# Joining the triangular inverses of two successive scan steps in one group of 64x64 products

## The chip, the cores and the metric

The kernel runs on one core of one Trainium2 chip. The metric is the time of one execution on the device in microseconds (us). A core has a matrix engine (PE, with its weight loads shown apart as PEld), a vector engine (DVE), a scalar engine (ACT), a general engine (POOL), and a queue processor (SP) that issues most of the transfers (DMA) between main memory and the on-chip memory. Each engine carries out its own list of instructions strictly in the order of that list. Matrix products end in PSUM, a memory of eight banks, from which DVE and ACT fetch them.

## The reference, cut to what matters

One layer mixes tokens in two ways, a gated delta rule and a windowed attention. The change lies in the delta rule. For each chunk of 64 tokens it needs the inverse of a unit lower triangular matrix, and then a scan over the chunks:

```python
a_mat = jnp.where(strict, jnp.einsum('nbhik,nbhjk->nbhij', kb, kc) * decay, 0.0)
t_mat = lax.linalg.triangular_solve(a_mat, eye, left_side=True, lower=True, unit_diagonal=True)
u = jnp.einsum('nbhij,nbhjv->nbhiv', t_mat, vc * bc[..., None])
w = jnp.einsum('nbhij,nbhjk->nbhik', t_mat, kb * jnp.exp(gc)[..., None])
def step(s, xs):
    v_new = u_n - jnp.einsum('bhck,bhkv->bhcv', w_n, s)
    s_new = s * jnp.exp(gl_n)[..., None, None] + jnp.einsum('bhck,bhcv->bhkv', kd_n, v_new)
    o = jnp.einsum('bhck,bhkv->bhcv', qd_n, s) + jnp.einsum('bhij,bhjv->bhiv', qk_n, v_new)
```

It runs forwards and backwards over 2048 latent tokens behind 256 context tokens, with 4 heads of 128 columns.

## The kernel before, in words

The kernel works on chunks of 128 tokens instead of 64, so the scan has 18 steps, each with a forward (d = 0) and a backward (d = 1) chain. DVE makes the inverses of the two 64x64 diagonal blocks of each 128x128 matrix earlier and spills them. `merge` joins two such inverses into one of 128x128 by the rule for block triangular matrices, which takes two 64x64 products per head and direction, one after the other: the off-diagonal block times the inverse of one diagonal block (line 1021 for d = 0 and 1023 for d = 1, into PSUM tiles `myp`), a scaling and copy out of PSUM (lines 1025 and 1026), and the inverse of the other block times that (lines 1028 and 1030, into `mep`), copied into place by ACT with a minus sign (lines 1032 and 1033).

In detail `merge` clears a tile `mx0` and a tile `mx1` on POOL (line 991), loads the diagonal inverses into them (line 1002) and the off-diagonal blocks into `moff0` and `moff1` (line 1004), and turns them by PE transposes into `mtp` (line 1011 for d = 0, whole; line 1013 for d = 1, the lower 64 rows alone). For d = 0 the result is the tile `mw`, for d = 1 it is `mx1` itself. `mx0`, `mx1`, `mw`, `moff0` and `moff1` have two buffers each. The helper `in_step` makes the four heads' products follow each other so that products which use different quarters of PE's 128x128 array stand side by side in PE's list: 64 rows by 64 columns each.

`chain` carries the state: `ksps` (line 1093), a DVE update of `x` (1095), `vps` = joined inverse times `x` (1099), DVE's `v3` (1102), `sps` (1111), and DVE's new state (1117). `output` makes the chunk's output (1135 to 1147), `finalize` its norm and gate. In `scan`, the chains of step `st` are written first, then `merge` for step `st + 1`, then the outputs. The last two steps' inverses come late, from `base4`, a DVE job that is spread over the scan.

The scan stands beside `gates`, dense products of 128x128 weights with 512 columns (lines 524 to 526, PSUM tile `rps`), which need nothing of the scan. A scheduler lays down every engine's list when the kernel is built: the scan is marked as urgent, and gate products are put where its chains would leave PE empty. What is left of them goes on into the next stage, the attention (scores `sc`, line 910; transposes `pt`; weighted sums `av`; a copy `avt`, line 951, ends a unit; 32 units), and the projections (`pps`, line 1231) follow, held back until the eighth unit is done.

## Time and profile before

| | us |
|---|---|
| median of 3 runs (2003.56 to 2009.0) | 2004.95 |
| profiled execution, first to last instruction | 2004.9 |
| first transposes of `merge` | 920.1 |
| last transposes of `finalize` | 1345.3 |
| first attention score | 1358.2 |
| last gate product | 1436.0 |
| first projection | 1481.1 |

The profile is one execution. A row of a timeline gives start, duration, engine, line, operation, the tiles written and read, the shape, the count, and in brackets the idle time before and what ended it. The durations of PE's products overlap, since a product is still in flight when the next one starts: what a product costs PE is the distance from its start to the next one's. A product of two plain fp32 tiles stands as two instructions in the profile, a transpose or a gate product as one. A row of windows gives the busy time of each engine in that stretch and, behind it, the clock that TensorE was granted.

### The profile page before, as it was taken

How to read it: one execution, taken by the hardware profiler on the slowest of the kernel's cores; microseconds unless marked ns; L12 is line 12 of the kernel's file. 1: busy time of each engine (PE TensorE's matmuls, PEld its weight loads, DVE VectorE, ACT ScalarE, POOL GpSimd, SP SyncE). 2: the span in 40 equal slices, each digit the busy share in tenths (PEclk: the TensorE clock that was granted, in tenths of full speed). 3: DMA queues.
4: the chain of work that ended last, by engine and by line, in shares of the span. 5: the costliest groups of instructions: out<-in, count | busy, mean ns of one | idle time of the engine just before them, and what ended most of it. 6: DMA issues, size and time to landing. Idle time of an engine off the chain costs nothing. (4 is left out here: it accounts for less than half of the span.)

```text
span 2004.9 us, 32107 instructions
## 1 busy us (share of the span) xinstructions
PE 1921.2 (96%) x10947; PEld 1611.0 (80%) x10947; DVE 1509.2 (75%) x2871; ACT 807.4 (40%) x1998; POOL 692.6 (35%) x768
## 2 busy tenths in 40 slices
PE   6999999989999999999999999999989999999998
PEld 3888888779998778877888888788768888877786
DVE  6979766667776899999777776535587777747888
ACT  5755545554444322111222233224675655532221
POOL 1652210225543202004222233323456444420675
PEclk8999999999999999999999999999999999999999
DMA  7542326764546733537887777755355555456454
GB/s 252 175 127 94 98 87 154 184 162 157 161 143 166 189 113 113 142 90 216 225 255 221 224 213 217 193 176 165 126 187 173 176 162 165 129 165 211 137 169 136
DMA packets 387704, 333.12 MB, mean 166 GB/s; under 512 B 83993, under 2 KB 307537, under 8 KB 386901
## 3 DMA queue, kind: packets, MB, share of 16 engines
q1 hardware_dynamic: 352244, 288.60, 49.9%
q10 hardware_dynamic: 35296, 42.48, 6.0%
q8 instruction: 87, 1.43, 0.3%
q14 instruction: 77, 0.62, 0.1%
HBM read 220.28 MB, written 109.13 MB: 164 GB/s over the span
## 5 line engine op out<-in xcount | busy, mean ns | idle before, releaser
L524 PE MATMUL rps<-hh,wh 128*128 128x512 f32 x768 | 309.6, 403 | 5.0 <-DVE rt L818 3.8
L526 PE MATMUL rps<-hh,wl 128*128 128x512 f32 x768 | 309.0, 403 | 0.0
L525 PE MATMUL rps<-hl,wh 128*128 128x512 f32 x768 | 307.7, 401 | 0.0
L563 DVE SCALAR_TENSOR_TENSOR cacc<-y,cw,cacc 128x512 f32<-128x512 f32 (+1 forms) x224 | 163.2, 750 | 22.9 <-ACT cacc L561 18.9
L524 PEld LDWEIGHTS rps<-hh,wh 128*128 128x128 f32 x768 | 145.7, 190 | 39.8 <-DVE rt L818 4.3
L525 PEld LDWEIGHTS rps<-hl,wh 128*128 128x128 f32 x768 | 145.8, 190 | 32.7
L526 PEld LDWEIGHTS rps<-hh,wl 128*128 128x128 f32 x768 | 145.7, 190 | 32.8
L524 PE MATMUL lps<-hh,wh 128*128 128x512 f32 (+1 forms) x448 | 171.6, 383 | 0.2 <-ACT y L634 0.2
L525 PE MATMUL lps<-hl,wh 128*128 128x512 f32 (+1 forms) x448 | 171.3, 382 | 0.0
L526 PE MATMUL lps<-hh,wl 128*128 128x512 f32 (+1 forms) x448 | 171.2, 382 | 0.0
L945 DVE TENSOR_TENSOR pl<-pt,ph 128x512 fp32r<-128x512 f32 x156 | 105.4, 685 | 41.9 <-ACT ph L943 41.2
L943 ACT CAST ph<-pt 128x512 fp32r<-128x512 f32 x156 | 90.2, 585 | 109.9 <-PE pt L941 76.8
L917 DVE CUSTOM_DVE_ANT_0 pr<-sc,band,sk 128x640 f32<-128x640 f32 (+1 forms) x128 | 106.6, 862 | 34.4 <-PE sc L913 18.3
L816 ACT ACTIVATE rt<-rps 128x512 f32<-128x512 f32 x96 | 57.3, 596 | 181.6 <-PE rps L526 167.8
L749 DVE TENSOR_TENSOR N<-N,btmp 128x62 f32<-128x62 f32 (+30 forms) x124 | 117.2, 945 | 3.0
L747 DVE TENSOR_TENSOR btmp<-N 128x62 f32<-128x62 f32 (+30 forms) x124 | 116.6, 940 | 3.1
L927 POOL TENSOR_SCALAR pr<-pr,sm 128x640 f32<-128x640 f32 (+1 forms) x128 | 99.7, 799 | 55.5 <-DVE sm L925 39.0
L919 ACT ACTIVATE pr<-pr,sm 128x640 f32<-128x640 f32 (+1 forms) x128 | 104.0, 815 | 20.4 <-DVE sm L917 20.4
L246 DVE TENSOR_TENSOR wl<-wr,wh 128x512 fp32r<-128x512 f32 x120 | 92.7, 786 | 24.7 <-POOL wh L245 21.9
L1231 PE MATMUL pps<-yh,wph 128*128 128x512 f32 x256 | 104.8, 411 | 4.3 <-ACT yh L1211 2.2
L245 POOL TENSOR_SCALAR wh<-wr 128x512 fp32r<-128x512 f32 x72 | 48.6, 690 | 170.3 <-PE lps L525 97.2
L1232 PE MATMUL pps<-yl,wph 128*128 128x512 f32 x256 | 100.9, 396 | 0.0
(374 smaller groups left out, 5044.2 us busy)
## 6 DMA issues: line engine op xcount, KB each, us to landing
wr<-in_w_in_dram SPq DMA_DIRECT2D x120, 256.0 KB
kw<-Ksp SPq DMA_DIRECT2D x28, 384.0 KB
x<-vsp SPq DMA_DIRECT2D x36, 256.0 KB
k<-ksp SPq DMA_DIRECT2D x34, 256.0 KB
kT<-kTsp SPq DMA_DIRECT2D x34, 256.0 KB
wm<-in_w_mod_dram SPq DMA_DIRECT2D x16, 512.0 KB
xt<-in_x_dram SPq DMA_DIRECT2D x16, 512.0 KB
dtl<-Dsp SPq DMA_DIRECT2D x32, 256.0 KB
```

Of the source, the lines that this page charges most:

```text
L524: T.matmul(ps, lhsT=wh[:, k], rhs=xh[:, k], start=k == 0, stop=False)
L525: T.matmul(ps, lhsT=wh[:, k], rhs=xl[:, k], start=False, stop=False)
L526: T.matmul(ps, lhsT=wl[:, k], rhs=xh[:, k], start=False, stop=k == kt - 1)
L563: V.scalar_tensor_tensor(a, y[:, t:t + n], cw[:, m, t:t + 1], a, op0=ALU.mult, op1=ALU.add)
L747: V.tensor_tensor(tv, A[:, m + 1:, m].unsqueeze(2).to_broadcast([h1 + n, r, m]), A[:, m, 0:m].unsqueeze(1).to_broadcast([h1 + n, r, m]), o ...
L749: V.tensor_tensor(A[:, m + 1:, 0:m], A[:, m + 1:, 0:m], tv, op=ALU.add)
L917: V.tensor_tensor_reduce(s_, ps[:, o:768], band[:, b0:b0 + W + 256], -0.125, sk[:, 1, hd:hd + 1], ALU.add, ALU.min, sm[:, h, 1:2])
L919: S.activation(s_, s_, AF.Exp, scale=-1.0, bias=sm[:, h, 1:2], accum_out=sm[:, h, 2:3])
L927: G.tensor_scalar(p[:, h, :W + 256], p[:, h, :W + 256], sm[:, h, 3:4], 1.0, op0=ALU.mult, op1=ALU.mult)
L945: V.tensor_tensor(pl, pt, f32(ph), op=ALU.subtract)
L1231: T.matmul(ps, lhsT=wh[:, k, ms], rhs=hs[k], start=k == 0, stop=False)
L1232: T.matmul(ps, lhsT=wh[:, k, ms], rhs=ls[k], start=False, stop=False)
```

## The change

`merge` is cut in two. `halves_of` does what came ahead of the first products: loads, transposes, the copy to `mw`, and for d = 1 the scaling (line 1014 now), which writes into a free part of `mx0` instead of a tile of its own. The d = 1 transposes are whole 128x128 ones now. `joined` then takes the second products of a step whose first are done (`done`) and the first products of the step after it (`begun`), and hands all four kinds to `in_step` as one group: `mep` in rows 0 to 63 of the array and one PSUM bank, `myp` in rows 64 to 127 and another bank. Behind it ACT copies the finished inverse into place, and DVE and ACT prepare the next. The scan therefore starts `halves_of` two steps ahead instead of one, with the same two buffers for each tile. No instruction of other functions changes.

```diff
-    def merge(pool, cs):
+    def halves_of(pool, cs):
...
             for h in hs:
-                if d == 0:
-                    T.transpose(tps[:, h], Xs[0][:, h], ident)
-                else:
-                    T.transpose(tps[:, h, 64:128], Xs[1][64:128, h], ident[64:128, 64:128])
+                T.transpose(tps[:, h], Xs[d][:, h], ident)
             tp.append(tps)
         brb = [br[:, c, d * 4:d * 4 + 4].unsqueeze(2).to_broadcast([128, H, 64]) for d, c in enumerate(cs)]
-        y0, y1 = offs[0], pool.tile([128, H, 64], F32, name="my1")
         W, X = pool.tile([128, H, 128], F32, name="mw", bufs=2), Xs[1]
         S.copy(W, tp[0])
-        V.tensor_tensor(y1[64:128], tp[1][64:128, :, 64:128], brb[1][64:128], op=ALU.mult)
-        yps = [psum(f"mg{d}", [128, H, 128], name="myp") for d in range(2)]
-        in_step([lambda h: T.matmul(yps[0][0:64, h, 0:64], lhsT=offs[0][64:128, h], rhs=W[64:128, h, 64:128],
-                                    start=True, stop=True),
-                 lambda h: T.matmul(yps[1][64:128, h, 0:64], lhsT=offs[1][64:128, h], rhs=y1[64:128, h],
-                                    start=True, stop=True)])
-        V.tensor_tensor(y0[0:64], yps[0][0:64, :, 0:64], brb[0][0:64], op=ALU.mult)
-        S.copy(y1[0:64], yps[1][64:128, :, 0:64])
-        eps_ = [psum(f"mg{d}", [128, H, 128], name="mep") for d in range(2)]
-        in_step([lambda h: T.matmul(eps_[0][0:64, h, 0:64], lhsT=Xs[0][0:64, h, 0:64], rhs=y0[0:64, h],
-                                    start=True, stop=True),
-                 lambda h: T.matmul(eps_[1][64:128, h, 0:64], lhsT=y1[0:64, h], rhs=X[0:64, h, 0:64],
-                                    start=True, stop=True)])
-        S.activation(W[0:64, :, 64:128], eps_[0][0:64, :, 0:64], AF.Copy, scale=-1.0)
-        S.activation(X[64:128, :, 0:64], eps_[1][64:128, :, 0:64], AF.Copy, scale=-1.0)
-        return W, X
+        xt2 = Xs[0][64:128, :, 64:128]
+        V.tensor_tensor(xt2, tp[1][64:128, :, 64:128], brb[1][64:128], op=ALU.mult)
+        return W, X, Xs[0], offs, xt2, brb
+
+    def joined(done, begun):
+
+        products = []
+        if done:
+            W, X, X0, offs0, _, _ = done
+            y0, y1 = (o[0:64] for o in offs0)
+            eps_ = psum("mg0", [128, H, 128], name="mep")
+            products += [lambda h: T.matmul(eps_[0:64, h, 0:64], lhsT=X0[0:64, h, 0:64], rhs=y0[:, h],
+                                            start=True, stop=True),
+                         lambda h: T.matmul(eps_[64:128, h, 0:64], lhsT=y1[:, h], rhs=X[0:64, h, 0:64],
+                                            start=True, stop=True)]
+        if begun:
+            W2, _, _, offs, xt2, brb = begun
+            yps = psum("mg1", [128, H, 128], name="myp")
+            products += [lambda h: T.matmul(yps[0:64, h, 0:64], lhsT=offs[0][64:128, h], rhs=W2[64:128, h, 64:128],
+                                            start=True, stop=True),
+                         lambda h: T.matmul(yps[64:128, h, 0:64], lhsT=offs[1][64:128, h], rhs=xt2[:, h],
+                                            start=True, stop=True)]
+        in_step(products)
+        if done:
+            S.activation(W[0:64, :, 64:128], eps_[0:64, :, 0:64], AF.Copy, scale=-1.0)
+            S.activation(X[64:128, :, 0:64], eps_[64:128, :, 0:64], AF.Copy, scale=-1.0)
+        if begun:
+            V.tensor_tensor(offs[0][0:64], yps[0:64, :, 0:64], brb[0][0:64], op=ALU.mult)
+            S.copy(offs[1][0:64], yps[64:128, :, 0:64])
...
-        W = merge(pool, [orders[d][0] for d in range(2)])
+        begun = halves_of(pool, [orders[d][0] for d in range(2)])
+        joined(None, begun)
+        done, begun = begun, halves_of(pool, [orders[d][1] for d in range(2)])
+        joined(done, begun)
         for st in range(NC):
+            W = done[:2]
             r = [chain(d, st, W[d]) for d in range(2)]
...
-            if st + 1 < NC:
-                W = merge(pool, [orders[d][st + 1] for d in range(2)])
+            done, begun = begun, halves_of(pool, [orders[d][st + 2] for d in range(2)]) if st + 2 < NC else None
+            if done:
+                joined(done, begun)
```

The scheduler's lists move with it. First place: PE's list in the middle of the scan, from the backward chain's `vps` to the transposes. The numbers behind `mx` tell the buffers' generations apart. Before:

```order
L1099 MATMUL vps<-x_10964,mw 128x128 x4
L1011 MATMUL mtp<-ident,mx_11038 128x128 x3
L1135 MATMUL aps<-S_10681,qT_10931 128x128 x4
L1099 MATMUL vps<-x_11002,mx_10868 128x128 x4
L1011 MATMUL mtp<-ident,mx_11038 128x128
L1013 MATMUL mtp<-ident,mx_11044 128x64 x4
```

And in the changed kernel, where 16 gate products stand in place of the line of dots:

```order
L1106 MATMUL vps<-x_11017,mx_10713 128x128 x4
L1008 MATMUL mtp<-ident,mx_11053 128x128 x4
...
L1153 MATMUL ops<-v_10865,qd_10948 128x128 x4
L1118 MATMUL sps<-v_10998,k_10977 128x128 x4
L1118 MATMUL sps<-v_11036,k_11015 128x128 x4
L1008 MATMUL mtp<-ident,mx_11059 128x128 x4
L1024 MATMUL mep<-moff_10884,mx_10880 64x64
L1026 MATMUL mep<-mx_10886,moff_10890 64x64
```

The d = 1 transposes (`mx_11059`) stood right behind `vps` and now stand 16 gate products, one `ops` and two `sps` later: their tile is the buffer that this very `vps` has just read (`mx_10713`). And one pair of `mep` products goes ahead of the group by itself.

Second place: PE's list at the groups of 64x64 products. Before, the second products of a step, eight together (its first products stand as such a group of eight a little earlier):

```order
L1093 MATMUL ksps<-S_11033,kT_11181 128x128 x2
L1028 MATMUL mep<-moff_11042,mx_11038 64x64
L1030 MATMUL mep<-mx_11044,my_11060 64x64
L1028 MATMUL mep<-moff_11042,mx_11038 64x64
L1030 MATMUL mep<-mx_11044,my_11060 64x64
...
L1146 MATMUL ops<-v_10985,qd_11090 128x128 x4
```

In the changed kernel, with two more rounds of the four in place of the dots:

```order
L1100 MATMUL ksps<-S_11048,kT_11193 128x128 x2
L1031 MATMUL myp<-mw,moff_11057 64x64
L1033 MATMUL myp<-mx_11053,moff_11063 64x64
L1024 MATMUL mep<-moff_10884,mx_10880 64x64
L1026 MATMUL mep<-mx_10886,moff_10890 64x64
...
L1031 MATMUL myp<-mw,moff_11057 64x64
L1033 MATMUL myp<-mx_11053,moff_11063 64x64
L1153 MATMUL ops<-v_11000,qd_11102 128x128 x4
```

Two groups of eight have become one of fourteen, behind a pair. In the whole list there were 41 unbroken runs of 64x64 products (36 groups, five of them with one product apart), and 18 blocks of 64-row transposes between whole ones; now there are 40 runs: 17 of fourteen, 13 pairs, 8 single products where a pair is broken by other work, and 2 groups of eight at the ends. The blocks of 64-row transposes are gone.

Third place: POOL's list, where the tiles are cleared ahead of their loads (line 989 now, 991 before; `x` times `rin` prepares the chains). Before:

```order
L1131 AFFINE_SELECT qd_11090<-qd_11090 128x512
L1086 TENSOR_TENSOR x_11140<-x_11140,rin 128x512
L991 MEMSET mx_11044 128x512
L1086 TENSOR_TENSOR x_11178<-x_11178,rin 128x512
L1131 AFFINE_SELECT qd_11109<-qd_11109 128x512
```

In the changed kernel:

```order
L1138 AFFINE_SELECT qd_11275<-qd_11275 128x512
L1093 TENSOR_TENSOR x_11325<-x_11325,rin 128x512
L989 MEMSET mx_11059 128x512
L1093 TENSOR_TENSOR x_11363<-x_11363,rin 128x512
L1138 AFFINE_SELECT qd_11294<-qd_11294 128x512
```

The place in POOL's list is the same, but `mx_11044` was read by transposes one step later, and `mx_11059` is read in the same step. Between the first transposes and the first attention score there are 991 gate products now, where there were 919; 120 are left behind that point, where there were 192. In the attention the last of them stands among the scores of the fifth unit of 32, where it was those of the seventh.

## The prediction

> **What bounds the kernel now.** I read the page's first part, then windows around the scan, then who waits for whom there. First the engines over the whole span:
>
> ```profile
> PE 1921.2 (96%) x10947; PEld 1611.0 (80%) x10947; DVE 1509.2 (75%) x2871; ACT 807.4 (40%) x1998; POOL 692.6 (35%) x768
> ```
>
> Then four windows, each with PE, PEld, DVE, ACT, POOL, the granted clock and DMA: the scan up to the first attention score, the attention while gate products last, four units of it without any, and two later units filled with projections:
>
> ```profile
> 920.00:1358.00 438.00, 427.35 (x3049) 369.60 (x3047) 298.37 (x707) 111.74 (x366) 139.95 (x218) 0.99 0.76 219
> 1358.00:1440.00 82.00, 81.97 (x440) 69.90 (x439) 47.19 (x109) 41.92 (x93) 28.37 (x35) 1.00 0.43 137
> 1440.00:1482.00 42.00, 34.86 (x184) 26.99 (x183) 34.25 (x77) 32.85 (x73) 26.64 (x27) 0.96 0.59 188
> 1550.50:1575.50 25.00, 25.00 (x144) 21.31 (x143) 18.34 (x42) 13.62 (x33) 11.01 (x12) 1.00 0.47 147
> ```
>
> PE is full wherever it has something to fill with. What it waits for in the scan:
>
> ```profile
> PE ksps L1093 <- DVE S L1117: 4.5, 1, 4.5
> PE ops L1146 <- DVE oa L1140: 1.8, 1, 1.8
> PE mep L1028 <- DVE moff L1025: 1.5, 1, 1.5
> ```
>
> These three are 7.8 us of 438. So the scan's chains set how long the stage is, gate products fill it, and a microsecond of PE's work saved there is worth one only if the filling left over is not missed later. The two windows of `rps` alone (counts of PEld, which has no missing records) tell how much fills each stage:
>
> ```profile
> 1358.00:1436.50 78.50, 48.85 (x194) 34.99 (x192) 0.00 (x0) 4.75 (x8) 1.00 0.42 132
> 920.00:1358.00 438.00, 241.52 (x921) 167.84 (x919) 10.20 (x15) 22.72 (x38) 0.99 0.76 219
> ```
>
> **The groups of 64x64 products.** A group between gate products in PE's timeline (start, duration):
>
> ```profile
> 925.53 0.40 PE L524 MATMUL rps<-hh,wh 128*128 128x512 f32 x1
> 925.77 0.39 PE L525 MATMUL rps<-hl,wh 128*128 128x512 f32 x1
> 926.09 0.27 PE L1021 MATMUL myp<-mw,moff 64*64 64x64 f32 x1
> 926.10 0.27 PE L1023 MATMUL myp<-my,moff 64*64 64x64 f32 x1
> 926.20 0.22 PE L1021 MATMUL myp<-mw,moff 64*64 64x64 f32 x1
> 926.20 0.22 PE L1023 MATMUL myp<-my,moff 64*64 64x64 f32 x1
> ...
> 926.55 0.22 PE L1021 MATMUL myp<-mw,moff 64*64 64x64 f32 x1
> 926.55 0.22 PE L1023 MATMUL myp<-my,moff 64*64 64x64 f32 x1
> 926.70 0.51 PE L526 MATMUL rps<-hh,wl 128*128 128x512 f32 x1
> 927.04 0.40 PE L524 MATMUL rps<-hh,wh 128*128 128x512 f32 x1
> ```
>
> A gate product takes 0.233 (925.53 to 925.77). From 925.77 to 927.04 are 1.27; less two gate products 0.80 for the group. Its eight slots, each with one instruction in either quarter, stand (926.55 - 926.20)/6 = 0.058 apart; so a run costs 0.33 for the change of mode and 0.058 per slot. Before: 41 runs, 36 x 8 slots and 10 more where one product stands apart, 298 slots: 41 x 0.33 + 298 x 0.058 = 30.8 us.
>
> Now there are 40 runs. That row and column quarters of different rows run at once no row shows: here both quarters share rows 64 to 127 and still start 0.01 apart. If four do as two do, the long runs take 8 slots (four `myp` rounds set them), pairs and single products 2: 17 x 8 + 21 x 2 + 2 x 8 = 194 slots, 24.5 us, 6.3 less. If pairs of different rows take turns, the long runs have 14 slots, 296 in all, 30.4 us, 0.4 less. I take the former, since one slot holds two quarters with hardly any of its 0.058 spent on the second.
>
> The Trainium skill has a rule against it: "TensorE: Matmul & The Clock Gate", section "Wait — 56ns, not 53.3ns?", says that starts never come closer than about 25 ns. By it a long run's 28 instructions would take 0.70 instead of 8 x 0.058 = 0.46, 4 us more in 17 runs, an estimate. The rows above, 0.01 apart and less, speak against it for different quarters.
>
> **The transposes.** Blocks of four and two, and the 64-row block that goes:
>
> ```profile
> 920.08 0.60 PE L1011 MATMUL mtp<-ident,mx 128*128 128x128 f32 x4
> 1139.79 0.38 PE L1011 MATMUL mtp<-ident,mx 128*128 128x128 f32 x2
> 1140.11 0.46 PE L1013 MATMUL mtp<-ident,mx 64*128 64x64 f32 x4
> 1140.49 0.50 PE L526 MATMUL rps<-hh,wl 128*128 128x512 f32 x1
> 1140.83 0.40 PE L524 MATMUL rps<-hh,wh 128*128 128x512 f32 x1
> ```
>
> A whole transpose costs (0.60 - 0.38)/2 = 0.11. The 64-row block costs 1140.83 - 0.233 - (1139.79 + 0.22) = 0.59; four whole ones cost 0.44. Over 18 blocks 2.7 us less. On DVE and ACT each instruction has a successor of the same size, so they change in order only.
>
> **Sum on PE:** 6.3 + 2.7 = 9.0 us less.
>
> **What it buys.** The two orders put 991 gate products before the first score instead of 919: 72 more, 72 x 0.233 = 16.8 us, taken from the attention. So the scan stage gets 16.8 - 9.0 = 7.8 longer, to about 446, and the attention starts as much later. It has 16.8 us less to fill with. A unit ends with a copy on ACT:
>
> ```profile
> L951 ACT COPY avt<-av x5: 583/584/587, 1440.1 to 1481.8; 64x512 f32<-64x512 f32 x5
> L951 ACT COPY avt<-av x3: 582/584/585, 1550.7 to 1575.2; 64x512 f32<-64x512 f32 x3
> ```
>
> Without filling a unit takes (1481.8 - 1440.1)/4 = 10.4. With 24 projection products of the gate products' size, PE full, it takes 12.25, so its own work is 12.25 - 5.6 = 6.7 and 3.7 us of PE are lost in a bare unit. Units with 24 gate products (the new order has 24 in each of the first three) stay full, as those projection units do. Then five bare units stand before the first projection where four stood: 3.7 us lost. At least none is lost, if the filling left over stretches; at most two units, 7.4. I take 3.7.
>
> **The load on the path.** `mx1` for step st + 2 takes the buffer that step st's `vps` reads, so clear, load and transposes now fit between that `vps` and the group on which the next step's inverse hangs. The same chain before, where it had a step's time, from DVE's reading of the finished `vps` to a load's arrival (POOL's multiply waits for one):
>
> ```profile
> 1100.77 0.69 DVE L1102 TENSOR_TENSOR v<-vps,brs 128x512 f32<-128x512 f32 x1 [0.20 <-PE vps L1099]
> 1100.77 0.32 SPq L1085 DMA_DIRECT2D x<-vsp  x1
> 1101.91 0.64 POOL L1131 TENSOR_SCALAR_AFFINE_SELECT qd<-qd 128x512 f32<-128x512 f32 x1 [7.13 <-DMA qd<-QDsp]
> 1102.49 0.53 POOL L991 MEMSET mx<- 128x512 f32 x1
> 1103.05 1.24 SPq L1002 DMA_DIRECT2D mx<-Xsp  x2
> 1103.90 1.04 POOL L1086 TENSOR_TENSOR x<-x,rin 128x512 f32<-128x512 f32 x1 [0.88 <-DMA x<-vsp]
> ```
>
> The clearing is done 2.3 after `vps`, the second load issued by 3.5; a load issued at 1100.77 was there at 1103.90 at the latest, 3.1 for four times the bytes. So 3.5 - 0.6 + 3.1 = 6.0 at most. The new order leaves four transposes, 16 gate products, an `ops` and two `sps`. Plain products cost:
>
> ```profile
> 1065.24 1.05 PE L1146 MATMUL ops<-v,qd 128*128 128x128 f32 x8
> 1066.13 1.95 PE L1111 MATMUL sps<-v,k 128*128 128x128 f32 x16
> ```
>
> (1.95 - 1.05)/8 = 0.11 each instruction, so the cover is 0.44 + 3.73 + 24 x 0.112 = 6.9. It just holds. I take 0.1 per step, 1.7 us: between nothing (it holds always) and 1 us per step (POOL's queue holds the clearing up). Queued behind the waiting clearing on POOL is `x` times `rin` of the next backward chain, behind the load on SP `qd` and the next `k`, all needed half a step later.
>
> The stalls of PE on DVE (7.8 us above) will be dealt out anew; they may all go or double. I take them as they are.
>
> **The sum:** 2004.9 (span; the median of the runs is 2004.95) - 9.0 + 3.7 + 1.7 = 2001.3 us.
>
> **Rivals.** *Taking turns:* quarters of different rows do not overlap; 5.9 us come back: 2007.2. For it, no row shows such an overlap; against it, the starts 0.01 apart. The issue floor of the Trainium skill's page on the clock gate, named above, would be a milder form of it, 2005.4 by the estimate there.
>
> *The load comes late* (the slower side): `mx1` is cleared late since POOL's list is blocked by a wait ahead of it, and PE's list waits at the d = 1 transposes in every step. For it:
>
> ```profile
> POOL qd L1131 <- DMA qd<-QDsp: 90.0, 23, 7.8
> ```
>
> POOL was blocked 23 times by this load alone, 3.9 on average. Against it: the memset's place behind `x` is unchanged, and in the list of PE's waits in this stage no load stands. It decides from the point where the clearing starts more than 6.9 - 0.5 - 0.6 - 3.1 = 2.7 after `vps` (1.7 here). A stall also costs clock. The only long one:
>
> ```profile
> 1269.86 2.08 PE L1093 MATMUL ksps<-S,kT 128*128 128x128 f32 x8 [4.46 <-DVE S L1117]
> 1269.00:1276.00 7.00, 6.14 (x23) 5.62 (x24) 6.05 (x19) 1.98 (x9) 5.47 (x9) 0.52 0.93 250
> ```
>
> Behind 4.5 us of waiting stood 7.0 us at 0.52, 3.4 lost. At 0.9 a step and one such loss of clock: 17 x 0.9 + 3.4 - 1.7 = 17 more, 2018.
>
> *Everything is bought:* the filling left over reaches as far as before and no unit is barer, the load always holds: 2001.3 - 3.7 - 1.7 = 1995.9. For it, units with few gate products are still above 10.4; against it, five whole units without filling in the new order.
>
> **Chances and range.** Forecast 0.58, taking turns 0.12, late load 0.16, all bought 0.14. A measurement tells 0.3%, 6.0 us, from no change: faster is below 1998.9, slower above 2011.0. The redealt stalls give the forecast some 5 us either way: 0.30 faster, 0.66 same, 0.04 slower. Taking turns: 0.05, 0.75, 0.20. Late load: none, 0.25, 0.75. All bought: 0.75, 0.25. That makes 0.29 faster, 0.55 same, 0.16 slower; the order of everything after the scan moves too, which no row prices, so I round towards the sides: 0.31, 0.50, 0.19. The range of 8 in 10 is 1993 to 2014: below it a part of all bought with luck in the stalls, above it most of late load.
>
> **What would show it.** Right: in a long run, four starts within 0.02 and rounds 0.12 apart; `mtp` 36 x 4 whole, no 64-row ones; first score near 1368 and 120 gate products behind it, the last ends near unit three; bare units of 10.4, five of them; first projection near 1477. Wrong: starts of `myp` and `mep` 0.06 apart (taking turns); idle time before `mtp` or `myp` put down to DMA or POOL (late load); a clock below 0.99 in the scan. A time off by more than 5 us with all of these right would mean that DVE's stalls, not PE's work, set this stage.

## The result, and the profile after

The changed kernel takes 2016.3 us in the median of 4 runs (2013.1 to 2016.5) where the kernel before took 2006.2 in 4 runs beside them: 1.0063 times as long, 95% interval 1.0046 to 1.0079. It got slower, where 2001.3 us was forecast and up to 2014 held possible. A repeat of both on another chip gave 1.0065 (1.0041 to 1.0088).

The profiled execution of the changed kernel, first part of its page:

```profile
span 2011.4 us, 32057 instructions
PE 1914.5 (95%) x10947; PEld 1603.1 (80%) x10947; DVE 1503.2 (75%) x2871; ACT 807.1 (40%) x1998; POOL 694.9 (35%) x768
```

This execution was the shortest of the four. PE is busy 6.7 us less than before (1921.2) and the span is 6.5 longer (2004.9): PE waits 13.2 us more. The windows by stage (length, then PE, PEld, DVE, ACT, POOL, granted clock, DMA), the scan first, then the attention up to the first projection, and the six units of it without gate products (their last 2.3 us hold first projections already):

```profile
919.00:1383.10 464.10, 440.45 (x3120) 379.78 (x3119) 293.47 (x710) 113.57 (x369) 146.04 (x223) 0.98 0.74 212
1383.10:1488.20 105.10, 99.66 (x545) 81.75 (x544) 78.62 (x180) 72.71 (x160) 52.13 (x57) 1.00 0.53 164
...
1433.90:1490.50 56.60, 51.16 (x281) 39.82 (x281) 51.92 (x114) 46.59 (x101) 35.77 (x38) 1.00 0.59 179
```

The scan is 464.1 us long (438.1 before) and PE idles 464.10 - 440.45 = 23.7 us in it (10.7 before). The attention up to the first projection is 105.1 (123.0 before). What follows is as long as it was: 523.2 against 523.8. So the loss lies in the scan. Gate products in the two stages, as forecast, 991 and 120 (column PEld):

```profile
919.00:1383.10 464.10, 263.94 (x992) 182.79 (x991) 10.19 (x15) 24.69 (x41) 0.98 0.74 212
1383.10:1431.00 47.90, 30.81 (x121) 21.68 (x120) 0.00 (x0) 2.98 (x5) 1.00 0.46 142
```

What PE waits for in the scan now, its own rows before `mtp` and the longest other one (sum, times, longest):

```profile
PE mtp L1008 <- DMA mx<-Xsp: 7.1, 6, 4.9
PE mtp L1008 <- POOL mx L996: 5.0, 2, 4.4
PE mtp L1008 <- POOL wh L245: 4.4, 1, 4.4
PE vps L1106 <- ACT mw L1037: 1.9, 1, 1.9
PE mtp L1008 <- POOL x L1093: 1.1, 1, 1.1
```

The transposes `mtp` at the head of `halves_of`, for which PE waited not once before, stand for 17.6 us in ten waits. Three of these, of 4.9, 4.4 and 4.4 us, make 13.7 of them; none of the others is longer than 1.1. By the tile that the transposes read (ACT's copy to `mw` follows those of `mx0`), 5.2 us fall to the load of `mx0`, 7.5 to that of `mx1` and 5.0 to copies of `base4`, the job that supplies the last steps' inverses. All other waits shrank from 10.2 to 5.8. The clock pays again for the long ones, in three stretches of the changed kernel's scan, where there were two in the scan before:

```profile
987.60:994.40 6.80, 5.58 (x16) 4.55 (x17) 0.69 (x1) 2.12 (x6) 2.04 (x2) 0.50 0.86 255
1028.60:1035.30 6.70, 5.77 (x17) 4.83 (x18) 6.33 (x17) 0.00 (x0) 3.26 (x4) 0.50 0.58 163
1264.10:1270.90 6.80, 4.92 (x18) 4.44 (x19) 4.33 (x10) 0.80 (x2) 3.58 (x6) 0.50 0.89 295
```

```profile
1156.30:1159.60 3.30, 3.30 (x11) 2.72 (x11) 3.27 (x12) 0.08 (x1) 0.00 (x0) 0.50 0.84 209
1268.90:1275.70 6.80, 5.84 (x22) 5.36 (x23) 6.15 (x19) 1.98 (x9) 5.17 (x9) 0.50 0.93 251
```

Half clock costs half of the time that PE worked in it (its idle part is counted as idle time already): now (5.58 + 5.77 + 4.92)/2 = 8.1 us, before (3.30 + 5.84)/2 = 4.6 in the scan and 3.17/2 = 1.6 in the attention (1446.4 to 1449.8, granted clock 0.50). The balance of scan and attention, with PE's own work as what remains of the time without idle time and half clock:

| us | before | changed | difference | forecast |
|---|---|---|---|---|
| PE idle in the scan | 10.7 | 23.7 | +13.0 | +1.7 |
| half clock in the scan | 4.6 | 8.1 | +3.5 | 0 |
| PE idle in the attention | 7.2 | 5.4 | -1.8 | +3.7 |
| half clock in the attention | 1.6 | 0 | -1.6 | 0 |
| PE's own work | 537.0 | 532.0 | -5.0 | -9.0 |
| scan and attention | 561.1 | 569.2 | +8.1 | -3.6 |

(The span grew by 6.5 only, since the scan began 1.1 earlier and what follows is 0.6 shorter.)

The longest wait is for `mx0`: its clearing on POOL, the transfer that held SP's list, the load, PE's transposes and the ACT copy that reads them:

```profile
977.45 0.53 POOL L989 MEMSET mx<- 128x512 f32 x1
980.29 3.68 SPq L1002 DMA_DIRECT2D moff<-offsp  x1
984.07 1.27 SPq L1000 DMA_DIRECT2D mx<-Xsp  x2
988.82 1.09 PE L1008 MATMUL mtp<-ident,mx 128*128 128x128 f32 x4 [4.88 <-DMA mx<-Xsp]
990.00 0.59 ACT L1012 COPY mw<-mtp 128x512 f32<-128x512 f32 x1 [5.05 <-PE mtp L1008]
```

The buffer was clear at 978.0. SP's list came to the load at 984.1, 6.1 us later: ahead of it stood other transfers, of which the load of a `moff` waited 3.7 us by itself until the step's `vps` had ended.

The next long wait is for `mx1`. In order of time: the last `vps` that reads the old `mx1`, the clearing on POOL, SP's list, and the transposes that need the new `mx1`:

```profile
1016.04 0.83 PE L1106 MATMUL vps<-x,mx 128*128 128x128 f32 x6
1016.86 2.14 SPq L1092 DMA_DIRECT2D x<-vsp  x1
1016.99 0.53 POOL L989 MEMSET mx<- 128x512 f32 x1 [10.58 <-ACT v L1114]
1019.09 0.99 SPq L1136 DMA_DIRECT2D qd<-QDsp  x1
1020.18 0.45 SPq L1092 DMA_DIRECT2D x<-vsp  x1
1020.72 0.38 SPq L1158 DMA_DIRECT2D osp<-oa  x1
1021.19 3.05 SPq L1000 DMA_DIRECT2D mx<-Xsp  x2
1029.53 1.08 PE L1008 MATMUL mtp<-ident,mx 128*128 128x128 f32 x4 [4.38 <-POOL wh L245]
```

POOL clears at once: 1016.99, 0.1 behind the end of `vps`. The tile is clear at 1017.5, but SP's list has four other transfers ahead of the load and comes to it at 1021.2, 3.7 us later; the second half is issued by 1024.2 and PE goes on at 1029.5. (The wait is put down to a POOL instruction, since that one came last, but its clearing of `mx` was long done; what was still missing is the load.) The second half came so late since its issue waited 1.8 us for another transfer. PE goes on 12.7 us behind the end of `vps`; it had work for 8.3 of them and stood still for 4.4.

### The profile page after: what moved, and what is told of

The parts are those of the page before. It is cut to its first block, busy times and chain, and to the rows that moved or that the text cites. A ratio compares the mean times of both kernels' runs of the same rounds, so it can differ in the third digit from the quotient of the medians.

```text
span 2011.4 us, 32057 instructions
## 1 busy us (share of the span) xinstructions
PE 1914.5 (95%) x10947; PEld 1603.1 (80%) x10947; DVE 1503.2 (75%) x2871; ACT 807.1 (40%) x1998; POOL 694.9 (35%) x768
## 5 line engine op out<-in xcount | busy, mean ns | idle before, releaser
L945 DVE TENSOR_TENSOR pl<-pt,ph 128x512 fp32r<-128x512 f32 x156 | 105.1, 684 | 36.2 <-ACT ph L943 35.5
L919 ACT ACTIVATE pr<-pr,sm 128x640 f32<-128x640 f32 (+1 forms) x128 | 104.0, 815 | 15.9 <-DVE sm L917 15.8
```

The lines of the kernel that those rows point to most:

```text
L919: S.activation(s_, s_, AF.Exp, scale=-1.0, bias=sm[:, h, 1:2], accum_out=sm[:, h, 2:3])
L945: V.tensor_tensor(pl, pt, f32(ph), op=ALU.subtract)
```

## The experiments

They ran on other chips, on which the kernel before takes about 2001 us; every ratio is against runs of the kernel before on the same chip. The table has each kernel's profiled execution (busy time, and span less busy time), PE's waits in the scan, before `mtp` and all others, and into how many runs the order breaks the 64x64 products.

| kernel | ratio (95%) | PE busy | PE idle | waits before mtp | other waits | runs |
|---|---|---|---|---|---|---|
| before, again | 0.9990 (0.9977 to 1.0003) | 1916.9 | 82.2 | 0.0 | 8.7 | 41 |
| changed, again | 1.0065 (1.0041 to 1.0088) | 1921.2 | 97.0 | 17.6 | 6.5 | 40 |
| a_qt | 1.0048 (1.0029 to 1.0066) | 1915.9 | 91.4 | 12.7 | 7.8 | 39 |
| a_three | 1.0084 (1.0071 to 1.0097) | 1915.2 | 100.3 | 8.3 | 16.8 | 50 |
| a_base | 1.0034 (1.0022 to 1.0047) | 1912.4 | 95.3 | 18.2 | 6.0 | 40 |
| a_apart | 1.0082 (1.0069 to 1.0096) | 1922.2 | 92.0 | 11.8 | 9.1 | 53 |
| a_all | 1.0074 (1.0053 to 1.0095) | 1916.2 | 92.2 | 12.9 | 14.5 | 35 |
| a_once | 1.0037 (1.0019 to 1.0054) | 1912.1 | 95.3 | 15.4 | 5.7 | 38 |
| a_first | 1.0037 (1.0020 to 1.0054) | 1907.2 | 95.9 | 10.7 | 10.0 | 21 |
| a_first_base | 1.0032 (1.0021 to 1.0044) | 1905.2 | 98.5 | 16.4 | 8.5 | 19 |
| a_pool | 1.0038 (1.0024 to 1.0051) | 1915.3 | 89.1 | 1.8 | 13.8 | 40 |
| a_pool_base | 1.0022 (1.0007 to 1.0037) | 1913.9 | 88.1 | 1.2 | 11.2 | 41 |
| a_pool_first_base | 0.9969 (0.9956 to 0.9983) | 1906.9 | 91.1 | 12.8 | 3.9 | 19 |
| a_mix_first_base | 0.9993 (0.9976 to 1.0010) | 1907.3 | 93.3 | 1.4 | 16.3 | 20 |
| b_one | 1.0182 (1.0161 to 1.0203) | 1930.6 | 109.2 | 12.9 | 8.5 | 53 |
| b_whole | 1.0000 (0.9985 to 1.0015) | 1915.7 | 85.6 | 3.8 | 12.5 | 42 |
| b_base | 1.0038 (1.0022 to 1.0055) | 1918.7 | 86.8 | 0.0 | 15.9 | 39 |
| b_pool | 1.0072 (1.0054 to 1.0090) | 1925.8 | 85.0 | 1.1 | 14.3 | 60 |

PE busy contains half clock, which differs by some us from one execution to the next; the ratios come from 4 to 12 runs each, the other columns from one. Names with a_ start from the changed kernel, with b_ from the kernel before.

**Is it the buffer?** The first theory: `mx1` can be loaded only once the step's `vps` has read its buffer, and a third buffer gives the load a step's time again. A rival: `base4` supplies the last two steps' inverses too late, now that they are wanted a step earlier; the transposes waited 4.4 us for one of its copies (timeline of the changed kernel):

```profile
1263.95 0.61 POOL L996 COPY mx<-x 64x256 f32<-64x256 f32 x1 [2.08 <-DMA x<-X4sp]
1265.98 1.11 PE L1008 MATMUL mtp<-ident,mx 128*128 128x128 f32 x4 [4.44 <-POOL mx L996]
```

*a_three*, and *a_qt*, which has its second line alone:

```diff
-            X = pool.tile([128, H, 128], F32, name=f"mx{d}", bufs=2)
+            X = pool.tile([128, H, 128], F32, name=f"mx{d}", bufs=2 + d)
...
-            qT4 = pool2.tile([128, H, 128], F32, name=f"qT{d}", bufs=2)
+            qT4 = pool2.tile([128, H, 128], F32, name=f"qT{d}", bufs=1)
```

> The changed kernel with three buffers for mx1 instead of two (and one for qT in place of two, to make room for it), so that mx1 of step st + 2 no longer takes the buffer that step st's vps reads. If the load on the path made the change slower, PE no longer waits for DMA or POOL before the d = 1 transposes: the idle time of 5.2 and 4.8 us before mtp near 984 and 1025 goes, and with it the half clock behind it (3.4 us each), the first score comes 15 us earlier or more (some of that because the new order leaves 96 more gate products to the attention), and the whole takes 2000 to 2006 us. If base4's inverses, which are now wanted one step earlier, made it slower, the idle time of 4.7 us near 1261 stays and the whole takes 2013 to 2017. If neither load nor inverses but the grouping in quarters was the loss, it stays at 2016 or above, since the order now breaks the groups into 50 runs instead of 40, about 3 us more.

> The changed kernel with one buffer for qT in place of two and nothing else: what the run with three buffers for mx1 gave up to make room. All theories expect 2014 to 2019 us, as the changed kernel, with the waits for mx in place; if it moves by more than 5 us, the run with three buffers has to be read against this one.

Measured: 1.0084 and 1.0048, so the third buffer of `mx1` brought no gain in time. PE's two longest waits in the scan of a_three, by kind:

```profile
PE mtp L1008 <- DMA mx<-Xsp: 8.3, 3, 4.6
PE ops L1153 <- DVE oa L1147: 5.0, 3, 2.1
```

The waits before `mtp` halve, and those for `mx1` are gone (7.5 us in the changed kernel). The long ones that are left, 4.6 us at 995.5 and 3.1 at 1020.2, are before the transposes of `mx0`, which kept two buffers; the expectation above, like the one of a_pool below, takes the changed kernel's longest wait for one of `mx1`. With a third buffer the load of `mx1` is in time, then, but the whole gained nothing: the order laid down anew has 50 runs of 64x64 products instead of 40 and fewer gate products in the scan (895 instead of 991), and other waits, of DVE above all, rose from 5.8 to 16.8 us. A third buffer for `mx0` and `mx1` both was not tried.

*a_base*:

```diff
-            if m % 6 == 5:
+            if m % 8 == 7:
```

> The changed kernel with the interleaved work of base4 taken every 6th column turned to every 8th, so that the inverses of the last two steps are on their way earlier. If their being wanted one step earlier is part of the loss, the step from the 14th to the 15th inverse shrinks from 47.6 us to 25 or less, the idle time of 4.7 us near 1261 with its half clock goes, and the whole takes 2006 to 2011 us; the stalls of the first steps stay. If the load on the path is all of it, these gates move within the order only and the whole stays within 2013 to 2019.

Measured: 1.0034 (1.0022 to 1.0047), some 0.3% less than the changed kernel's 1.0065. The step from the 14th to the 15th inverse did shrink, from 47.6 us to 19.8 (starts of `vps` for d = 0), and the wait at 1261 went; but the waits before `mtp` add up to 18.2 as before, all but 2.2 of them for the load. So this copy of base4's was one source of waiting, and the new list has others in its place.

*a_apart* takes the groups apart, with `halves_of` two steps ahead as in the changed kernel:

```diff
-        in_step(products)
+        if done:
+            in_step(seconds)
+        if begun:
+            in_step(products)
```

> The changed kernel, still working two steps ahead with the same buffers, but with the products of the step that is ended and of the step that is begun listed as two groups, so that no group has four quarters of different rows. If the loss is the load on the path, mtp still waits for mx, and the whole takes 2016 to 2024 us (the groups cost PE about 6 us more, of which the filling hides a part). If the grouping itself did harm, it comes back to 2004 to 2008.

Measured: 1.0082, and 11.8 us of waits before `mtp`. The grouping is not the loss: without it the load is late all the same, and PE's own work in scan and attention, reckoned as in the balance, is 542.1 us (573.6 less 27.6 of idle time and 3.9 of half clock) instead of 532.0.

**Does a load in this place cost in the kernel before, too?** *b_one*:

```diff
-            X = pool.tile([128, H, 128], F32, name=f"mx{d}", bufs=2)
+            X = pool.tile([128, H, 128], F32, name=f"mx{d}", bufs=1)
```

> The kernel before with one buffer instead of two for mx0 and for mx1: the inverses are still joined one step ahead in two separate groups, but mx1 can only be loaded once the step's vps has read it. If a load that has to fit between vps and the next transposes is what costs, PE's idle time in the scan stage grows from 10.7 us to 25 or more, with waits before mtp put down to DMA or POOL, and the whole takes 2015 to 2035 us where the kernel before takes 2005. If the loss came with the grouping or with the new order of the list alone, the idle time stays near 11 and the whole within 2000 to 2010.

Measured: 1.0182. PE waits 12.9 us before `mtp`, where the kernel before waits not at all. The scan's window of b_one:

```profile
918.00:1430.00 512.00, 477.78 (x3240) 408.60 (x3238) 297.48 (x713) 120.67 (x382) 153.12 (x233) 0.96 0.69 199
```

The idle time in the scan is 34.2 us, more than the load's waits: its steps got so long that all gate products were used up (the last one ends 28 us ahead of the first score), and behind that nothing fills the scan's own waits. So the load's place costs without the grouping and without two steps' lead, but this run has a second loss in it.

**Was the kernel before a lucky list?** Any edit makes the scheduler lay down every list anew. *b_whole* takes the d = 1 transposes whole, and *b_base* has base4's line of a_base:

```diff
-                if d == 0:
-                    T.transpose(tps[:, h], Xs[0][:, h], ident)
-                else:
-                    T.transpose(tps[:, h, 64:128], Xs[1][64:128, h], ident[64:128, 64:128])
+                T.transpose(tps[:, h], Xs[d][:, h], ident)
```

> The kernel before with the d = 1 transposes taken whole and nothing else: PE's work gets 2.7 us less and the list is laid down anew, with all loads a step ahead as before. If waits for loads make the changed kernel slower, PE's idle time in the scan stage stays at 8 to 14 us here and the whole takes 1996 to 2004 us (2000.6 to 2006 for the kernel before). If the 10.7 us of idle time before are a lucky draw, and any new list idles some 20 us as the four runs so far did (20.8 to 25.3), the whole takes 2008 to 2016.

> The kernel before with base4's work taken every 8th column instead of every 6th, and nothing else; the scan gets about 17 us shorter and the attention is left 72 gate products more. If waits for loads that have a step's time make no idle time, PE's idle time in the scan stage is 8 to 14 us and the whole takes 1996 to 2005. If the kernel before is a lucky draw among lists, it is about 20 us and the whole takes 2008 to 2016.

Measured: 1.0000 and 1.0038, idle times in the scan of 16.4 and 16.2 us, between the two theories. With the load a step ahead no PE wait falls to it (b_whole's 3.8 are a copy of base4's), but other waits, most of them for DVE, are 8.7, 12.5 and 15.9 us in the three lists. So the kernel before idles least among three lists of its kind. That some 5 us of the difference to the changed kernel are such a draw is likely by this, but not shown.

*a_all* puts third buffer, base4's line and the order of a_first (below) together:

> The changed kernel with three edits together: three buffers for mx1 (one for qT), base4's work every 8th column, and in each group the products of the step that is begun listed ahead of those of the step that is ended, by which 35 runs of 64x64 products remain instead of 50 with three buffers alone. If load and late inverses are the loss, neither wait is left, the idle time in the scan stage is 15 us or less, and with 9 us less of PE's work the whole takes 1994 to 2002 us. If a list that works two steps ahead idles 20 us or more whatever its buffers, it takes 2006 to 2014.

Measured: 1.0074, 12.9 us before `mtp` and 14.5 of other waits, together the most in the table. A third buffer for `mx1` doesn't repair the loads here either; `mx0` kept its two, and which tile each wait was for is not told apart.

**What holds the load up: POOL's list, SP's list, or the transfer?** *a_once* clears `mx0` and `mx1` once, ahead of the scan, in fixed buffers:

```diff
-            X = pool.tile([128, H, 128], F32, name=f"mx{d}", bufs=2)
-            G.memset(X, 0.0)
+            X = cleared[d][orders_[d].index(c) % len(cleared[d])]
...
+        for d in range(2):
+            cleared.append([pool.tile([128, H, 128], F32, name=f"mx{d}{i}") for i in range(2 + 0)])
+            for X in cleared[d]:
+                G.memset(X, 0.0)
```

> The changed kernel with mx0 and mx1 held in two fixed buffers each that are cleared once ahead of the scan instead of in every step (outside of the diagonal blocks nothing but the finished block is ever written there, so the zeros last). The load still waits for the step's vps and still goes through SP's list, but no longer waits for POOL. If POOL's list is what makes the load late, the idle time before mtp goes and the whole takes 2000 to 2006 us. If it is SP's list, the waits stay, shorter by the 0.5 us of the clearing, and the whole takes 2010 to 2017.

Measured: 1.0037, the waits before `mtp` still 15.4 us:

```profile
PE mtp L1010 <- DMA mx<-Xsp: 9.8, 4, 7.4
PE mtp L1010 <- POOL mx L998: 5.6, 2, 4.2
```

With no clearing to wait for the load is as late as before, the longest wait even longer. POOL's list is not the cause.

*a_pool* leaves the clearing and issues the load from POOL's list, right behind it:

```diff
-                    dma(X[b * 64:b * 64 + 64, :, b * 64:b * 64 + 64], Xsp[d][c][:, b].rearrange("h r c -> r h c"))
+                    G.dma_start(X[b * 64:b * 64 + 64, :, b * 64:b * 64 + 64], Xsp[d][c][:, b].rearrange("h r c -> r h c"))
```

> The changed kernel with the loads of mx0 and mx1 issued by POOL, right behind the clearing in POOL's own list, instead of by SP; buffers and program order are as in the changed kernel. In that kernel's trace the clearing starts at once when vps has read the buffer (984.05, 1016.99), and the load is issued 4 us later, behind moff, zasp, wr and x in SP's list. If that place in SP's list is what makes the load late, PE's idle time before mtp falls from some 20 us to 8 or less and the whole takes 2000 to 2008 us. If the transfers themselves are slow, since the DMA engines are busy, the idle time stays and the whole takes 2012 to 2020. If POOL's list is blocked by waits for x and qd ahead of the clearing, it gets worse: above 2020.

Measured: 1.0038, and 1.8 us of waits before `mtp` instead of 17.6. The same step as above, in a_pool:

```profile
1017.12 0.83 PE L1106 MATMUL vps<-x,mx 128*128 128x128 f32 x6
1018.06 0.53 POOL L989 MEMSET mx<- 128x512 f32 x1 [3.12 <-issue]
1018.88 1.26 POOL L1000 DMA_DIRECT2D mx<-Xsp  x2 [0.29 <-POOL mx L989]
1026.02 0.60 PE L1008 MATMUL mtp<-ident,mx 128*128 128x128 f32 x4
```

The buffers, the clearing and the size of the transfer are those of the changed kernel. The load is issued 0.3 us after the clearing instead of 3.7, and PE reaches the transposes 8.1 us after `vps` without any wait. So what made the load late was its place in SP's list. That isn't the whole loss: 0.4% of the 0.65% stayed. Other waits rose at the same time (13.8 instead of 5.8 to 6.5, most of them for DVE), and the attention of a_pool has 4.9 us of half clock by the reckoning above, where the changed kernel has none:

```profile
1374.38:1479.68 105.30, 97.15 (x521) 80.66 (x520) 77.99 (x180) 71.95 (x159) 52.41 (x57) 0.95 0.50 156
```

(base4's wait went with the new list too, though the edit doesn't touch it.)

*a_pool_base* adds base4's line:

> The changed kernel with the loads of mx issued by POOL and base4's work every 8th column: both suspected waits taken away with two buffers as before. If the place in SP's list and the late inverses are all of the loss, the idle time in the scan stage is 12 us or less and the whole takes 1995 to 2001 us. If a list laid out two steps ahead idles 20 us whatever feeds it, it takes 2006 to 2014.

Measured: 1.0022, the idle time in the scan 12.4 us. The interval reaches from just above the kernel before to that of a_pool, so what base4's line adds isn't told apart here.

*b_pool*, the same edit in the kernel before, with the two repeats of the unchanged kernels beside it:

> The kernel before with the loads of mx0 and mx1 issued by POOL instead of SP. There the load has a step's time and no wait of PE hangs on it. If the load's place in SP's list matters only where it has to fit between vps and the next transposes, nothing is gained: 1998 to 2008 us (its list breaks the groups into 60 runs instead of 41, 6 us more of PE's work, and fills the attention instead of the scan). If POOL's list is the better place as such, it gets faster than before by 0.3% or more, below 1995.

> The kernel before, unchanged, profiled on the chip of the runs beside it. If the chip alone is 5 us faster, the ratio is 1.000 and PE's idle time in the scan stage is 6 to 12 us, without any wait before mtp for SP or POOL. If 10.7 us were luck of one execution, it is 14 or more.

> The changed kernel, unchanged, on the same chip. If the loss lies in the lists and not in the chip, the ratio is 1.005 to 1.008 again, some 2010 to 2016 us, with about 20 us of idle time in the scan stage, most of it before mtp. If it were an effect of the first chip, the ratio is below 1.003.

Measured: 1.0072 for b_pool, so POOL's list is no better place for this load as such. What its trace shows is a new list with 60 runs of 64x64 products (PE busy 8.9 us more than in the repeat of the kernel before; 19 more runs at 0.33 would be 6.3) and 14.3 us of waits for others. The repeats gave 0.999 and 1.0065. Scan and attention of the kernel before, again:

```profile
919.60:1354.60 435.00, 426.07 (x3048) 368.95 (x3047) 298.23 (x707) 111.70 (x366) 138.53 (x218) 0.99 0.77 221
1354.60:1476.50 121.90, 115.12 (x618) 94.95 (x616) 80.41 (x184) 74.06 (x163) 54.98 (x61) 1.00 0.49 155
```

and of the changed kernel on the same chip:

```profile
918.00:1383.60 465.60, 441.19 (x3120) 380.91 (x3119) 293.11 (x710) 113.48 (x369) 145.72 (x223) 0.98 0.73 211
1383.60:1489.10 105.50, 99.67 (x546) 81.80 (x545) 78.52 (x180) 72.52 (x160) 51.98 (x57) 1.00 0.52 163
```

Idle time in the scan 8.9 and 24.4, in the attention 6.8 and 5.8, half clock 3.4 and 9.5, own work 537.8 and 531.4: +15.5, -1.0, +6.1 and -6.4, the balance of the first pair once more. The waits before `mtp` fall to the same three again, 5.8 us for `mx0`'s load, 7.0 for `mx1`'s and 4.8 for base4's copies.

**Can the change pay?** *a_first* lists the first products of the begun step ahead of the second ones of the ended step, so that each group stays whole:

```diff
-        in_step(products)
+        in_step(products + seconds)
```

> The changed kernel with the first products of the step that is begun listed ahead of the second products of the step that is ended, so that 21 runs of 64x64 products remain instead of 40: 19 changes of mode fewer at 0.33 us, and 17 runs of 8 slots with four quarters, 6 to 7 us less of PE's work. The loads are as in the changed kernel. If a run costs what the prediction says, PE's own work falls by 6 to 7 us; if the load on the path is what remains, the waits before mtp stay and the whole takes 2006 to 2014 us.

Measured: 1.0037. With 21 runs instead of 40 PE's own work in scan and attention is 526.6 us (559.5 less 29.8 of idle time and 3.1 of half clock), 5.4 less than 532.0 where 6 to 7 were expected. Of these, 2.0 are slots (all runs together take 11.1 us from first to last start in the changed kernel, 9.1 here), so these 19 changes of mode cost some 0.2 us each, not 0.33. Waits before `mtp` stay, 10.7 us. *a_pool_first_base* has all three: load on POOL's list, base4's line, whole groups:

> The changed kernel with three edits: loads of mx issued by POOL, base4's work every 8th column, and the first products listed ahead of the second, which leaves 19 runs of 64x64 products instead of 41. Against the run with the first two edits alone (1.0022 times before) PE's own work falls by the 4 to 7 us that fewer runs save. If PE's work counts once the load is no longer waited for, it takes 1996 to 2000 us, as fast as the kernel before or up to 0.2% faster; if another wait takes its place, it stays at 2003 or above.

Measured: 0.9969 (0.9956 to 0.9983): 1995.2 us where the kernel before takes 2001.8, faster than both. *a_first_base* is the same kernel with the load back on SP's list, and *a_mix_first_base* has it there for the two context steps alone:

```diff
-                    G.dma_start(X[b * 64:b * 64 + 64, :, b * 64:b * 64 + 64], Xsp[d][c][:, b].rearrange("h r c -> r h c"))
+                    (G.dma_start if c >= NCB else dma)(X[b * 64:b * 64 + 64, :, b * 64:b * 64 + 64], Xsp[d][c][:, b].rearrange("h r c -> r h c"))
```

> The changed kernel with the first products listed ahead and base4's work every 8th column, but with the loads of mx on SP's list as in the changed kernel. If the load's place in SP's list goes on costing, PE waits 12 us or more before mtp for SP, and the ratio to the kernel before is 0.999 to 1.003, against 0.997 with the load on POOL's list. If with the two other edits the load is no longer late, it is 0.997 or less.

> The three edits together, but with the loads of mx for the two context steps on SP's list and only the later ones on POOL's. If the late start of the scan costs, the first vps comes 8 to 10 us earlier and the ratio falls from 0.997 to 0.993 to 0.996; if the gates that fill that gap are only put elsewhere, it stays at 0.996 to 0.999.

Measured: 1.0032 and 0.9993. So issuing the load from POOL, with the new lists that come of it, is worth 0.6% in this kernel, and the intervals lie far apart. How much of that is the load's place is not shown: the same edit took 0.3% off the changed kernel and 0.1% off a_base, and a new list alone moved the time by 0.4% in b_base. PE's waits for this load in the scan of a_first_base:

```profile
PE mtp L1008 <- DMA mx<-Xsp: 12.5, 7, 4.6
```

and of a_pool_first_base:

```profile
PE mtp L1008 <- DMA mx<-Xsp: 8.9, 4, 5.3
```

PE is busy as long (1905.2 and 1906.9); the waits in the scan are 16.7 us instead of 24.9, and of these 8.2 only 3.6 lie before `mtp`. The two profiled executions are 5.7 us apart, the medians 13.7 (1995.2 and 2008.9), so the traces show less than half of the difference. And the load is not always in time from POOL's list either (one wait of 5.3), while in a_mix_first_base, where it is (1.4), other waits took its place (16.3). How these share out among DVE, ACT and POOL from list to list wasn't settled.

## Why the prediction was wrong, point by point

**PE's work:** the mechanism was right, the size roughly. 9.0 us less were forecast; by the balance 5.0 and 6.4 came in the two pairs, each from single executions, and why it is less is not shown. The runs of 64x64 products themselves take 17.3 us from first to last start before and 11.1 in the changed kernel, 6.2 less; the 104 slots fewer were to save 104 x 0.058 = 6.0. In a long run of the changed kernel (timeline) the four quarters start within 0.03 us of each other, the slots stand 0.058 apart, and 28 instructions take 0.47 us:

```profile
1075.49 0.27 PE L1031 MATMUL myp<-mw,moff 64*64 64x64 f32 x1
1075.50 0.27 PE L1033 MATMUL myp<-mx,moff 64*64 64x64 f32 x1
1075.51 0.27 PE L1024 MATMUL mep<-moff,mx 64*64 64x64 f32 x1
1075.52 0.27 PE L1026 MATMUL mep<-mx,moff 64*64 64x64 f32 x1
1075.60 0.22 PE L1031 MATMUL myp<-mw,moff 64*64 64x64 f32 x1
...
1075.66 0.22 PE L1031 MATMUL myp<-mw,moff 64*64 64x64 f32 x1
...
1075.96 0.22 PE L1033 MATMUL myp<-mx,moff 64*64 64x64 f32 x1
1076.11 0.38 PE L1153 MATMUL ops<-v,qd 128*128 128x128 f32 x1
```

The rival that they take turns is refuted, and so is its milder form: 28 starts in 0.47 us are 0.017 apart.

**What it buys:** the mechanism was right, the term was not. 991 and 120 gate products came as forecast, so the attention had 16.8 us less to fill with. But it got 17.9 us shorter, 3.4 of that by less idle time and half clock, so nothing was lost there. There are six bare units instead of the five forecast. They ended 9.4 us apart, (1490.5 - 1433.9)/6, with 0.9 us idle each (56.60 - 51.16 over six), not 3.7. The 3.7 were already too much for the kernel before: its row for the four bare units, 34.86 busy of 42.00, leaves 1.8 each, and 0.4 more of the 10.4 are half clock (1.6 us over four).

**The load on the path:** this is the step that failed: "It just holds. I take 0.1 per step, 1.7 us." Where SP's list was free it nearly held: most loads were issued within 1 us of their clearing, and PE waited 1.1 us at most for them. It failed in three places, by three sources, of which the sum priced one. In the wait shown for `mx1` the cover was judged well (6.9 us; 8.3 there), the need was not (6.0; 12.7). The row that priced it, a load issued 2.3 us after `vps`, was taken where SP's list was free. Here the clearing came even sooner, but four transfers stood ahead of the load, 3.7 us, its two halves took 3.0 to issue, and the second was there 5.3 later, against 3.5 for clearing and both issues and 3.1 for the transfer in the estimate. The load of `mx0`, two steps ahead now and held up in the same list, made the longest wait, and base4's copies another of 4.4; both were put at nothing, and so was the half clock behind a wait. Measured against the 1.7 us are 17.6 of waits before `mtp` (7.5 for `mx1`, 5.2 for `mx0`, 5.0 for base4) and 3.5 to 6.1 more of half clock, less 2 to 4 that other waits became shorter. What else of the time comes from the lists being laid anew stays open: with the load in time, a_pool still takes 0.4% more than the kernel before.

**PE's other waits,** taken as unchanged at 7.8 and a few tenths, went from 10.2 to 5.8 and from 8.7 to 6.5: right in size. That they can double, as allowed for, b_base and a_three show.

**The rivals:** the late load was the one that came, with 2018 against 2016.3 measured, and was given 0.16. Its place (waits before `mtp`, half clock behind) was right and its trigger wrong: not a clearing later than 2.7 us behind `vps` by a blocked POOL list (it came 0.1 behind), but SP's list. That its time came so close is partly luck: it counted 0.9 us of `mx1`'s load in each of 17 steps, and what came were three long waits for three different tiles. Its 3.4 us of clock also count some idle time twice (0.86 of the 7.00 us of its row). One of the three, base4's copies, now wanted one step earlier, the prediction didn't name: 4.4 us and 2.5 of clock, and a_base, which removes this wait, moved the time by some 0.3%.

The prediction named two of the signs that came, idle time before `mtp` and a clock below 0.99 in the scan. Their chance was set too low, since the price of a wait was taken without what the clock adds and without looking up what stands ahead of the load in the new SP list, though that list was there to be read.

## What to carry to other kernels

When a change takes away the step of slack that a load had, what counts is not the transfer's time but every instruction that stands ahead of it in its issuing queue's new list: read that list between the release of the buffer and the load, sum it with the waits in it, and do so for every load that the change hurries, not for the nearest one alone. A load that depends on something one engine does last can be issued from that engine's own list; here this took the waits away in one kernel (a_pool), and with whole groups and base4's line it went with the step from 0.3% slower to 0.3% faster. And where a scheduler lays down every list anew, an edit elsewhere moved this kernel by 0.4% too (b_base): an effect of that size needs a run that undoes one part.

## What was not expected of the hardware

How long PE may stand still before its clock is halved. Over the 20 traces, gaps between two starts on PE in the scan were compared with the clock behind them (the waits in the rows are 0.2 to 0.4 us shorter than these gaps): of 121 gaps of 0.9 to 2.0 us one was followed by half clock (in b_one, behind its last gate product), of 39 between 2.0 and 3.4 us 21 were, and 31 of 32 longer ones; the last lies within a stretch of half clock. The half clock lasted 3.4 or 6.8 us, in b_one also 10.2 and 27.3. A busy PE loses half of that, so by these figures a gap of 2 us can cost 2 + 1.7 = 3.7 us, and one of 5 us some 8, an estimate. The Trainium skill, "TensorE: Matmul & The Clock Gate", Part 1, says that the clock drops after an idle window of about 3.4 us and that the window runs freely. The lengths of 3.4 us agree with such a window; that gaps of 2.0 to 3.4 us were enough half the time does not agree with a window that has to be idle from end to end.

Products in four different quarters of PE's array start 0.01 us apart (rows at 1075.49 to 1075.52), and a fourth quarter costs a slot nothing: the 8 slots with two and with four quarters stand 0.058 apart alike.
